# First tiles of the first two experts limited to blocks 0 to 5 and computed unsplit beside the routing of the last blocks

## The chip, the cores and the metric

The kernel runs on one core of a Trainium2 chip. The metric is the device time of one execution in microseconds (us). Five engines work side by side, each with an instruction queue of its own that is worked off in order: TensorE (PE, matmuls; its weight loads are PEld), VectorE (DVE), ScalarE (ACT), GpSimd (POOL) and SyncE (SP, which issues most transfers). A compiler fixes the order within each queue ahead of time from a timeline that it simulates; on the chip, semaphores hold an instruction until its inputs are there.

## The reference, cut to what matters

One layer: attention and a state-space branch, merged and projected to `x`, then a mixture of experts on the normalised `x`. The change touches the second block only:

```python
def hierarchical_moe(h, ...):                        # 1024 tokens of width 1024
    g_prob, g_idx = top_k(softmax(ht @ w_group_router + group_bias), 1)      # one of 4 groups
    in_group = expert logits of that group                                   # 4 experts
    e_val, e_loc = top_k(softmax(in_group), 2)                               # two experts of 16
    gates = one_hot(e_glob) * g_prob * e_val / sum(e_val)
    a = einsum('td,edf->tef', ht, w_e_gate)          # 1024 -> 256
    u = einsum('td,edf->tef', ht, w_e_up)
    hid = silu(a) * u * gates[:, :, None]
    out = hid.reshape(t, 16 * 256) @ w_e_down        # 256 -> 1024
```

## The kernel before, in words

**Blocks.** The output projection runs over eight blocks of 128 tokens (loop `for b in range(8)`, lines 1225 to 1275). A block has two halves of 512 columns, and a half has eight steps of three matmuls, because a float32 product is made of three products of numbers split into a high and a low part (`woh`/`wol`, `mh`/`ml`). At fixed steps `(half, kb)` of this loop, pieces of the routing of earlier blocks are called: `x1_transpose` (the block's `x`, transposed), `logits` or, for blocks 0 to 5, `pair_logits` and `pair_sum` (two blocks at once, on split numbers), `choose` (the two experts of each token and their weights), `place` (each token's rank within its expert, from the running counts `cum`), `slots` (matmuls of one-hot matrices that add the tokens to the table `slot`) and `h2_store` (the normalised block to DRAM, for gathering).

**Tables.** `slot` holds, for each of 16 positions, columns of 128 token numbers and gate weights. A position is an expert's place in the table: positions 0 to 7 and 8 to 15 are two halves of the experts whose tokens never overlap; positions 0 and 8 belong to experts 0 and 4, known ahead. Ranks above the first 128 go to a second column (a rank over 191 of the first eight positions, over 127 of the others, is moved on by 64, so that the second column of positions 0 to 7 fills rows 0 to 63 and that of 8 to 15 rows 64 to 127). The other positions are sorted by their counts (`key`, `rank`, `OHP`), and the numbers of the experts in that order (`who`, `whoi`, lines 1316 to 1323) are read by SP to load the right weights.

**Tiles.** There are 21 tiles of up to 128 tokens: (0), (0, 8), (8), then (5), (13), (1), (1, 9), (9) and so on. A tile of one position is computed on split numbers (24 matmuls of 512 columns for gate and up, 12 for down, lines 1426 to 1428 and 1468 to 1470); a shared tile takes up to 64 second-column tokens of each of two positions and is computed on float32 as it is (lines 1423, 1464), both halves side by side. Each tile gathers its tokens from DRAM (line 1378, POOL), transposes them (1407), computes, gathers the rows of the output (1389), adds (1471) and scatters them back (1395). A gather of output rows waits for the scatters of those tiles that may hold the same tokens. Tiles (0), (0, 8) and (8) wait for the table of all eight blocks (lines 1290 to 1296).

**Buffers.** `s4` tiles come from a pool of 40 buffers of 4 KB a partition; expert weights take six (`load_expert`, line 1007 and 1011), their split versions twelve (`split`, lines 100 and 101). `x4` tiles come from a pool of seven during the blocks. Weights of position 0 are loaded after block `LB`, those of position 8 after the blocks.

Of the kernel before, what the change touches and what calls it, by code (L numbers as in the profile page):

```python
# [19 lines left out]
D = 1024  # L20
# [5 lines left out]
LB = 6  # L26
# [11 lines left out]
def hybrid_layer(ctx, tc, a, out):  # L38
# [1007 lines left out]
    rbias, rbias0 = rtile("rbias", [128, 24]), rtile("rbias0", [128, 24])  # L1046
# [4 lines left out]
    wr, wr0 = rtile("wr", [128, KB, 24]), rtile("wr0", [128, KB, 24])  # L1051
# [24 lines left out]
    pool.tensor_scalar(num[:, 8:], num[:, 8:], 4.0, None, op0=OP.subtract)  # L1076
    kofs = rtile("kofs", [128, 16])
# [18 lines left out]
    def x1_transpose(b, hf):  # L1096
        if b >= 6 and hf == 0:
            X1T[b] = x4([128, KB, 128], F32, "x1T")
        if b < 6 and b % 2 == 0:
# [5 lines left out]
        if b >= 6:  # L1105
            act.activation(X1T[b][:, 4 * hf:4 * hf + 4].rearrange("p k c -> p (k c)"), p, AF.Copy)
            return
        hi, lo = [t[:, :, 128 * (b % 2):128 * (b % 2) + 128] for t in X1T[b - b % 2, hf]]
        p = p.rearrange("p (k c) -> p k c", k=4)
        act.activation(hi, p, AF.Copy)  # L1110
        dve.tensor_sub(lo, p, f(hi))

    def logits(b, hf):
        if hf == 0:
            LG[b] = pst("lg", 2)
        for kb in range(4 * hf, 4 * hf + 4):
            pe.matmul(LG[b][:, :24], X1T[b][:, kb], wr[:, kb], start=(kb == 0), stop=(kb == 7))
# [61 lines left out]
    def place(b):  # L1179

        OH, mk, wx = CH.pop(b)
        r = LG.pop(b)[:, 32:48]
# [41 lines left out]

    for b in range(8):
# [3 lines left out]
        for half in range(2):  # L1229
            c = slice(512 * half, 512 * half + 512)  # L1230
            p = pst("mm", 3)
            for kb in range(KB):
# [6 lines left out]
                if step == (0, 6) and b:  # L1239
                    if b == 7:  # L1240
                        logits(6, 1)
                        choose(6)
                    h2_store(b - 1)
                if step == (1, 4):
                    x1_transpose(b, 0)
                if b >= 2 and b % 2 == 0:
# [8 lines left out]
                if b >= 3 and b % 2:  # L1255
# [5 lines left out]
                if step == (1, 5) and b == 7:  # L1261
                    place(6)
                if step == (1, 7) and b >= 6:
                    logits(b, 0)
# [16 lines left out]
    slots(7)  # L1281
    h2_store(7)

    sl = const.tile([128, 432], F32, name="sl")
    id0 = const.tile([128, 3], I32, name="id0")
    gh0 = const.tile([128, 3], F32, name="gh0")
    tx, te = rtile("tx", [128, 3]), rtile("te", [128, 3])
    dve.tensor_scalar(te[:, :1], slot[:, :1], 0.0, 4096.0, op0=OP.is_equal, op1=OP.mult)  # L1290
    dve.scalar_tensor_tensor(id0[:, :1], slot[:, :1], -1.0, te[:, :1], op0=OP.add, op1=OP.add)
    dve.tensor_copy(sl, slot)
    dve.tensor_add(tx[:, 1:2], sl[:, 1:2], sl[:, 73:74])
    dve.tensor_copy(tx[:, 2:3], sl[:, 72:73])
    dve.tensor_scalar(te[:, 1:], tx[:, 1:], 0.0, 4096.0, op0=OP.is_equal, op1=OP.mult)
    last_dve = dve.scalar_tensor_tensor(id0[:, 1:], tx[:, 1:], -1.0, te[:, 1:], op0=OP.add, op1=OP.add)
    cntp = pst("lg", 2)
    pe.matmul(cntp[:, :16], ones, cum, start=True, stop=True)
    key = const.tile([128, 16], F32, name="key")
    cnt = const.tile([128, 16], F32, name="cnt")  # L1300
    dve.scalar_tensor_tensor(key, cntp[:, :16], 8.0, kofs, op0=OP.mult, op1=OP.add)
    dve.tensor_sub(cnt, cntp[:, :16], eoff)
    ph4.close()


    ov = ctx.enter_context(tc.tile_pool(name="ovt", reuse_waits="tile", bufs=1))
    rank = ov.tile([128, 2, 7], F32, name="rank")
    ph5 = ExitStack()
    sm = ph5.enter_context(tc.tile_pool(name="sm", reuse_waits="tile", bufs=1))
    ps = ph5.enter_context(tc.tile_pool(name="ps5", reuse_waits="tile", bufs=1, space=bass.MemoryType.PSUM))  # L1310
    og = [sm.tile([128, D], F32, name=f"og{i}") for i in range(3)]
# [3 lines left out]
    gt, OHP = sm.tile(HE, F32, name="gt"), sm.tile(HE, F32, name="OHP")  # L1315
# [4 lines left out]
    who, whoi = sm.tile([128, 14], F32, name="who"), sm.tile([128, 14], I32, name="whoi")  # L1320
# [4 lines left out]
    dve.tensor_add(sl[:, 144:288], sl[:, 144:288], sl[:, 288:])  # L1325
    slv = sl[:, :288].rearrange("p (x h e c) -> p x h e c", x=2, h=2, c=9)
    prod, part = sm.tile([128, 2, 14, 7], F32, name="prod"), sm.tile([128, 2, 2, SHARED - 1], F32, name="part")
    tab = sm.tile([128, 2, 13 + SHARED], F32, name="tab")
# [9 lines left out]
    idp, tep = sm.tile([128, 13 + SHARED], I32, name="idp"), sm.tile([128, 13 + SHARED], F32, name="tep")  # L1338
    dve.tensor_scalar(tep, tab[:, 0], 0.0, 4096.0, op0=OP.is_equal, op1=OP.mult)
    dve.scalar_tensor_tensor(idp, tab[:, 0], -1.0, tep, op0=OP.add, op1=OP.add)  # L1340
    dve.tensor_copy(gh0[:, 0::2], slv[:, 1, :, 0, 0])
    dve.tensor_add(gh0[:, 1:2], sl[:, 145:146], sl[:, 217:218])
# [12 lines left out]
    def split_expert(e):  # L1355
# [5 lines left out]
        for t in RAW[e][1]:  # L1361
# [4 lines left out]
    tiles = [((p,), id0[:, c:c + 1], gh0[:, c:c + 1]) if len(p_) == 1 else (p_, id0[:, c:c + 1], gh0[:, c:c + 1])  # L1366
             for c, p_ in enumerate(((0,), (0, 8), (8,))) for p in p_[:1]]
# [7 lines left out]
    acc = []  # L1375
# [6 lines left out]
    def access(n, ins):  # L1382
        for m, o in acc:
            if m != n and not any(x // 8 == y // 8 and x != y for x in tiles[m][0] for y in tiles[n][0]):
                tc.declare_no_dep(ins.ins, o.ins, reason="other rows of the output")
        acc.append((n, ins))

    def gather_out(n):
        access(n, pool.indirect_dma_start(
# [4 lines left out]
    def scatter(n):  # L1394
        access(n, pool.indirect_dma_start(
# [81 lines left out]
    for p in seq[:2]:  # L1477
        if p not in RAW:
            RAW[p] = load_expert(number(p))
    xg.append(s4([128, D], F32, "xg"))  # L1480
    gather(0)
    last = gather(1)
    with tc.issue_after(last.ins):
        for t in xg[2:] + og:
            pool.memset(t, 0.0)
    with tc.issue_after(last_act.ins), tc.issue_after(last_dve.ins):
        parts = split_expert(seq[0])
        for _ in range(4):
            next(parts)
        xpose(0)  # L1490
        for _ in parts:
            pass
    for n in range(NT + 1):
        if n < NT:
# [6 lines left out]
            if not alone:  # L1501
                bg.append(split_expert(es[1]))
            elif i + 1 < 16 and not (i % 2 == 0 and es[0] < SHARED):
                bg.append(split_expert(seq[i + 1]))
# [5 lines left out]
            gate_up(n, (lambda: hid_t(n - 1)) if n else (lambda: None), pump)  # L1510
        else:
            hid_t(n - 1)
        if n:
            down(n - 1, pump)
        while bg:
            pump()
# [5 lines left out]
    ps = ph6.enter_context(tc.tile_pool(name="ps6", reuse_waits="tile", bufs=1, space=bass.MemoryType.PSUM))  # L1522

# [138 lines left out]
```

## Time and profile before

| | before |
|---|---|
| median of 3 runs | 1060.28 us (1060.02 to 1061.85) |
| the profiled execution | 1057.99 us |
| its span, first to last instruction | 1056.2 us |
| TensorE busy | 977.8 us, 93% of the span |
| VectorE, ScalarE, POOL busy | 616.4, 435.9, 252.9 us |
| mean granted TensorE clock | 0.969 of full |
| moved by DMA | 153.24 MB |

The span is what the trace shows; the execution's own time is 1.8 us longer, and the runs that were timed without a profile have a median 2.3 us above it. A busy TensorE is not TensorE at its peak, since matmuls are pipelined and their ends are modelled: the price of a matmul within a run of them is read from the distance between two starts.

### The profile page before, as it was taken

To read this page: it belongs to the slowest core of one execution; us is meant where nothing else is said; L and a number is where in the kernel's file an instruction comes from. 1 tells how busy PE (TensorE), PEld (TensorE's weight loads), DVE (VectorE), ACT (ScalarE), POOL (GpSimd) and SP (SyncE) were. 2 spreads that over 40 slices of the span, in tenths; PEclk is the share of its full clock that TensorE was granted. 3 is DMA by queue.
4 is the path that set the end of the run, shared out by engine and by line. 5 is a ranking of instruction groups with operands and counts; after the bars stand their busy time and mean duration, and the time that the engine had idled before them with its cause. 6 is when DMAs were issued, how large, how long until landed. Compare 5 with 4: busy or idle time off the path is not lost.

```text
span 1056.2 us, 14525 instructions
## 1 busy us (share of the span) xinstructions
PE 977.8 (93%) x5135; PEld 755.8 (72%) x5135; DVE 616.4 (58%) x1341; ACT 435.9 (41%) x757; POOL 252.9 (24%) x312
## 2 busy tenths in 40 slices
PE   6998899999899999999999999899976989999993
PEld 5786688887677767788888888688853665666551
DVE  5756775874856556252210434826677868788841
ACT  6512215234656566340121223433334546666710
POOL 1199503212000000000000212823335223233132
PEclk9999899999999998999999999999986999999996
DMA  8242214134545261242211112433575998989522
GB/s 277 95 132 82 83 41 122 60 84 126 135 104 126 70 180 31 88 119 64 60 40 31 50 41 85 159 121 119 174 265 199 344 379 281 392 273 365 211 93 101
DMA packets 100267, 153.24 MB, mean 145 GB/s; under 512 B 10421, under 2 KB 59097, under 8 KB 100185
## 3 DMA queue, kind: packets, MB, share of 16 engines
q1 hardware_dynamic: 90968, 126.52, 37.9%
q0 software_dynamic: 9072, 25.18, 6.5%
q8 instruction: 42, 0.69, 0.3%
q10 hardware_dynamic: 144, 0.52, 0.2%
q14 instruction: 41, 0.33, 0.1%
HBM read 121.36 MB, written 28.20 MB: 142 GB/s over the span
## 4 chain that ended last, share of the span: by engine, by line
PE 67%; DMA 8%; DVE 7%; issue 7%; POOL 6%; ACT 2%; SPq 1%; POOLq 0%; DVEq 0%
PE mm L899 22%; PE mm L636 3%; PE mm L638 3%; PE mm L637 3%; PE S L760 3%; PE o L807 3%; PE mm L1234 3%; PE mm L1235 2%; PE mm L1233 2%; PE h L1423 2%; DMA k<-hl 2%; PE pt L792 2%; PE h L1427 2%; PE h L1428 2%; PE h L1426 2%
## 5 line engine op out<-in xcount | busy, mean ns | idle before, releaser
L989 POOL TENSOR_TENSOR t<-t,am 128x512 f32<-128x512 f32 x14 | 21.4, 1548 | 378.4 <-DVE t L988 378.4
L101 DVE TENSOR_TENSOR w1l<-w1r,w1h 128x1024 fp32r<-128x1024 f32 x64 | 76.0, 1220 | 3.9 <-ACT w1h L100 3.9
L636 PE MATMUL mm<-qh,hh 128*128 128x512 f32 x192 | 77.1, 405 | 0.0
L637 PE MATMUL mm<-ql,hh 128*128 128x512 f32 x192 | 76.0, 396 | 0.0
L638 PE MATMUL mm<-qh,hl 128*128 128x512 f32 x192 | 75.4, 394 | 0.0
L970 ACT ACTIVATE tg<-mm,hb 128x512 f32<-128x512 f32 x24 | 16.4, 685 | 122.5 <-PE mm L899 122.5
L101 DVE TENSOR_TENSOR ful<-fur,fuh 128x1024 fp32r<-128x1024 f32 x11 | 13.5, 1225 | 89.4 <-ACT fuh L100 89.4
L100 ACT ACTIVATE w1h<-w1r 128x1024 fp32r<-128x1024 f32 x64 | 64.0, 1056 | 0.0
L773 DVE CUSTOM_DVE_ANT_0 sb<-S,bias 128x640 f32<-128x640 f32 (+4 forms) x64 | 40.8, 654 | 37.4 <-PE S L760 35.8
L899 PE MATMUL mm<-hh,fuh 128*128 128x512 f32 x192 | 59.5, 390 | 1.0 <-DVE yal L816 1.0
L899 PE MATMUL mm<-hh,ful 128*128 128x512 f32 x192 | 59.1, 389 | 0.0
L899 PE MATMUL mm<-hl,fuh 128*128 128x512 f32 x192 | 59.1, 389 | 0.0
L668 POOL TENSOR_TENSOR st<-st,nhalf 128x8 f32<-128x8 f32 x16 | 28.5, 1806 | 115.4 <-DVE st L666 115.4
L775 ACT ACTIVATE sb<-sb,mx 128x640 f32<-128x640 f32 (+4 forms) x64 | 44.2, 692 | 23.2 <-DVE mx L773 18.9
L1234 PE MATMUL mm<-wol,mh 128*128 128x512 f32 x128 | 51.1, 399 | 2.7 <-POOL wol L930 1.6
L1427 PE MATMUL h<-w1l,xh 128*128 128x512 f32 x128 | 52.8, 412 | 0.3 <-DVE w1l L101 0.3
L1426 PE MATMUL h<-w1h,xh 128*128 128x512 f32 x128 | 53.0, 414 | 0.0
L1428 PE MATMUL h<-w1h,xl 128*128 128x512 f32 x128 | 52.1, 407 | 0.0
L1233 PE MATMUL mm<-woh,mh 128*128 128x512 f32 x128 | 50.4, 393 | 1.0 <-ACT woh L929 1.0
L1235 PE MATMUL mm<-woh,ml 128*128 128x512 f32 x128 | 50.4, 395 | 0.0
L793 ACT ACTIVATE pt<-pt 128x512 f32<-128x512 f32 (+1 forms) x72 | 36.6, 520 | 21.3 <-PE pt L792 21.0
L1471 DVE TENSOR_TENSOR og<-y,og 128x512 f32<-128x512 f32 x42 | 27.8, 687 | 28.0 <-DMA og<-out_y,idp 15.8
(404 smaller groups left out, 2521.3 us busy)
## 6 DMA issues: line engine op xcount, KB each, us to landing
w1r<-in_weg SPq DMA_DIRECT2D x64, 256.0 KB
w1r<-in_weu SPq DMA_DIRECT2D x64, 256.0 KB
w2r<-in_wed SPq DMA_DIRECT2D x32, 512.0 KB
fur<-in_w_in SPq DMA_DIRECT2D x11, 512.0 KB
qr<-in_w_in SPq DMA_DIRECT2D x16, 256.0 KB
qs<-hl SPq DMA_DIRECT2D x32, 128.0 KB
k<-hl SPq DMA_DIRECT2D x16, 256.0 KB
hur<-in_w_branch SPq DMA_DIRECT2D x16, 256.0 KB
```

Of the source, the lines that this page charges most:

```text
L100: act.activation(hi, raw, AF.Copy)
L101: dve.tensor_sub(lo, raw, f(hi))
L636: pe.matmul(o[j], hh[kb][:, tsl], wh, start=(kb == 0), stop=False)
L637: pe.matmul(o[j], hh[kb][:, tsl], wl, start=False, stop=False)
L638: pe.matmul(o[j], hl[kb][:, tsl], wh, start=False, stop=(kb == 7))
L899: pe.matmul(p[half], ww[:, kb], hx[kb][:, 512 * half:512 * half + 512], start=(kb == 0 and n == 0), stop=(kb == nk - 1 and n == 2))
L1233: pe.matmul(p, mh[kb][:, tsl], woh[kb][:, c], start=(kb == 0), stop=False)
L1234: pe.matmul(p, mh[kb][:, tsl], wol[kb][:, c], start=False, stop=False)
L1235: pe.matmul(p, ml[kb][:, tsl], woh[kb][:, c], start=False, stop=(kb == 7))
L1426: pe.matmul(pv, hi[:, kb], wh, start=(kb == 0), stop=False)
L1427: pe.matmul(pv, hi[:, kb], wl, start=False, stop=False)
L1428: pe.matmul(pv, lo[:, kb], wh, start=False, stop=(kb == 7))
```

## The change

Blocks 4 and 5 are routed singly, as 6 and 7 were (`PAIRED = 4`). When block 5 is placed, the counts of positions 0 and 8 are raised to 128 if they are lower, so that tokens of blocks 6 and 7 go to the second column. The first tiles of the two positions then hold tokens of blocks 0 to 5 only, and their tables are read while block 7 is projected (`early_tables`). They are gathered, transposed and computed on float32 as it is, with the raw weights, in program order between the routing steps of block 7 and the loop of experts (`early_*`). The sorting of the other experts moves ahead of `slots(7)`. The loop starts with tile 2, the shared tile (0, 8); output rows of tile 3 are gathered behind tile 2's scatter. Weights of position 0 are loaded one block earlier.

```diff
-LB = 6
+PAIRED = 4
+EARLY = 6
+LB = 5
...
-        if b >= 6 and hf == 0:
+        if b >= PAIRED and hf == 0:
...
 def place(b):
...
         dve.tensor_add(cum, cum, mk)
+        if b == EARLY - 1:
+            n2 = LG_[:, 48:50]
+            pe.matmul(n2, ones, cum[:, 0:16:8], start=True, stop=True, skip_group_check=True)
+            bump = rtile("bump", [128, 2])
+            dve.scalar_tensor_tensor(bump[:1], n2[:1], -1.0, full[:1], op0=OP.mult, op1=OP.add)
+            dve.scalar_tensor_tensor(cum[:1, 0:16:8], bump[:1], 0.0, cum[:1, 0:16:8], op0=OP.max, op1=OP.add)
...
+    def early_tables():
+        te, tg = rtile("tee", [128, 2]), rtile("tge", [128, 2])
+        v = slot.rearrange("p (x e c) -> p x e c", x=3, c=9)[:, :, 0:16:8, 0]
+        dve.tensor_scalar(te, v[:, 0], 0.0, 4096.0, op0=OP.is_equal, op1=OP.mult)
+        dve.scalar_tensor_tensor(ide, v[:, 0], -1.0, te, op0=OP.add, op1=OP.add)
+        for i in range(2):
+            pool.indirect_dma_start(out=xg[i], in_=h2d[:128 * EARLY], ...)
...
+    def early_xpose(i):
+        XE[i] = (s4 if i else x4)([128, KB, 128], F32, "xT")
+        ... eight transposes of xg[i], two copies by ScalarE
+    def early_gate_up(i, after=None):
+        w = RAW[8 * i][0]
+        ...
+        for kb in range(KB):
+            with tc.issue_after(after.ins) if after is not None and kb > 1 else nullcontext():
+                pe.matmul(p.rearrange("p (g c) -> p g c", g=2), x[:, kb], w[kb // 2][:, :, kb % 2],
+                          start=(kb == 0), stop=(kb == 7))
+        ... gate and up as in gate_up, with ghe
+    def early_hid_t(i):
+        ... two transposes, one copy by ScalarE
+    def early_out(i):
+        OG[i] = s4([128, D], F32, "oge")
+        pool.memset(OG[i], 0.0)
+        g = pool.indirect_dma_start(out=OG[i], in_=out[:128 * EARLY], ...)
+    def early_down(i):
+        ... four matmuls on RAW[8 * i][1], two sums into OG[i], one scatter
...
+                if b > PAIRED:
+                    if step == (0, 1) and b > PAIRED + 1:
+                        slots(b - 2)
+                        if b - 2 == EARLY - 1:
+                            early_tables()
+                    if step == (1, 5):
+                        place(b - 1)
+                if b == 7 and step == (1, 1):
+                    early_xpose(0)
...
+    RAW[8] = load_expert(4)
+    for i in range(2):
+        early_out(i)
     x1_transpose(7, 1)
-    logits(7, 1)
+    early_gate_up(0, logits(7, 1))
     slots(6)
     last_act = choose(7)
+    early_xpose(1)
     place(7)
+    ... counts, key, rank, who, whoi (moved up)
+    slots(7)
+    h2_store(7)
+    early_hid_t(0)
+    early_gate_up(1)
+    early_down(0)
+    ... the tables of the other tiles
+    early_hid_t(1)
+    early_down(1)
...
-    gather(0)
-    last = gather(1)
+    gather(2)
+    last = gather(3)
...
-    for n in range(NT + 1):
+    for n in range(2, NT + 1):
...
-            gather_out(n)
+            if n != 3:
+                gather_out(n)
...
+        if n == 3:
+            gather_out(n)
```

## Rows read from the trace of the kernel before

**Rows 1.** The page's chain that ended last, by engine.
```profile
PE 67%; DMA 8%; DVE 7%; issue 7%; POOL 6%; ACT 2%; SPq 1%; POOLq 0%; DVEq 0%
```

**Rows 2.** Stretch: length, busy PE, PEld, DVE, ACT, POOL, clock, DMA share, GB/s.
```profile
780.00:790.00 10.00, 4.42 (x30) 3.23 (x29) 9.89 (x55) 3.78 (x7) 4.95 (x6) 0.81 0.77 299
790.00:800.00 10.00, 3.22 (x7) 1.36 (x7) 8.87 (x57) 3.99 (x5) 2.34 (x3) 0.50 0.14 38
800.00:810.00 10.00, 5.59 (x18) 4.30 (x19) 10.00 (x24) 3.69 (x5) 8.92 (x8) 0.50 0.61 172
840.00:870.00 30.00, 27.39 (x124) 21.81 (x123) 21.99 (x28) 14.63 (x20) 9.72 (x9) 0.94 1.01 386
890.00:920.00 30.00, 29.21 (x142) 21.68 (x140) 27.09 (x35) 17.69 (x25) 10.31 (x9) 1.00 1.02 368
930.00:1010.00 80.00, 80.00 (x381) 53.29 (x378) 66.96 (x84) 48.44 (x68) 22.34 (x16) 1.00 0.78 275
```

**Rows 3.** Instructions in order of time, TensorE: start, duration, engine, line, [idle before].
```profile
782.03 0.63 PE L1104 MATMUL tr<-ident,xr 128*128 128x128 f32 x4 [0.24 <-DVE cum L1189]
...
802.26 1.94 PE L1407 MATMUL tr<-ident,xg 128*128 128x128 f32 x8 [5.59 <-DMA xg<-h2d,id]
...
804.03 0.80 PE L1426 MATMUL h<-w1h,xh 128*128 128x512 f32 x1
...
815.23 2.79 PE L1423 MATMUL h<-w1r,xT 128*64 128x512 f32 x10
```

**Rows 4.** Instructions in order of time, TensorE: what its matmuls cost.
```profile
151.68 0.61 PE L507 MATMUL inc<-U,Tt 128*128 128x128 f32 x4
...
813.30 0.39 PE L1426 MATMUL h<-w1h,xh 128*128 128x512 f32 x1
...
814.00 0.39 PE L1426 MATMUL h<-w1h,xh 128*128 128x512 f32 x1
...
872.24 3.65 PE L1423 MATMUL h<-w1r,xT 128*64 128x512 f32 x16
```

**Rows 5.** Instructions in order of time, TensorE: logits of a pair and of one block.
```profile
758.37 0.28 PE L1126 MATMUL lg<-x1h,wrs 128*48 128x256 f32 x1
...
758.83 0.28 PE L1126 MATMUL lg<-x1h,wrs 128*48 128x256 f32 x1
...
769.66 0.62 PE L1136 MATMUL lg<-i,lgT 48*128 48x24 f32 x4
770.21 1.07 PE L1117 MATMUL lg<-wr,x1T 128*128 128x24 f32 x8
```

**Rows 6.** Instructions in order of time, POOL and VectorE during the last routing.
```profile
786.13 2.34 POOL L1221 TENSOR_TENSOR h<-h,grow 128x1024 f32<-128x1024 f32 x1 [0.90 <-ACT h L1220]
...
786.49 2.00 DVE L1194 TENSOR_SCALAR lin<-lin 128x2 f32<-128x2 f32 x1
...
797.36 1.29 POOL L1378 DMA_INDIRECT xg<-h2d,id  x1 [8.89 <-DVE id L1291]
...
798.22 0.15 DVE L1296 SCALAR_TENSOR_TENSOR id<-tx,te 128x2 int32<-128x2 f32 x1
```

**Rows 7.** Instructions in order of time: output rows of the first unshared tile.
```profile
841.91 1.01 POOL L1395 DMA_INDIRECT out_y<-og,id  x1 [0.31 <-issue]
...
851.89 0.99 POOL L1389 DMA_INDIRECT og<-out_y,idp  x1 [5.27 <-DMA out_y<-og,id]
...
859.51 1.29 DVE L1471 TENSOR_TENSOR og<-y,og 128x512 f32<-128x512 f32 x2 [2.99 <-DMA og<-out_y,idp]
...
860.35 0.47 PE L1468 MATMUL y<-w2h,hih 128*128 128x512 f32 x1 [2.31 <-ACT w2h L100]
```

**Rows 8.** Instructions in order of time: counts, expert numbers, first numbered weights.
```profile
792.92 0.17 DVE L1301 SCALAR_TENSOR_TENSOR key<-lg,kofs 128x16 f32<-128x16 f32 x1
...
802.89 0.74 DVE L1323 CAST whoi<-who 1x14 int32<-1x14 f32 x1
...
804.43 0.36 SPq L1007 DMA_DIRECT2D w1r<-in_weg  x1
```

More of the change, by code (lines that the diff above doesn't have):

```diff
@@ L2 @@
 from collections import deque
-from contextlib import ExitStack
+from contextlib import ExitStack, nullcontext
 import concourse.bass as bass
@@ L1116, in logits @@
         for kb in range(4 * hf, 4 * hf + 4):
-            pe.matmul(LG[b][:, :24], X1T[b][:, kb], wr[:, kb], start=(kb == 0), stop=(kb == 7))
+            mm = pe.matmul(LG[b][:, :24], X1T[b][:, kb], wr[:, kb], start=(kb == 0), stop=(kb == 7))
+        return mm
     def pair_logits(b, hf):
@@ L1223, in h2_store @@
         X1.pop(b)
+    ide = const.tile([128, 2], I32, name="ide")
+    ghe = const.tile([128, 2], F32, name="ghe")
+    def early_tables():
[4 more added lines that the diff above has]
+        for i in range(2):
+            pool.indirect_dma_start(
+                out=xg[i], out_offset=None, in_=h2d[:128 * EARLY],
+                in_offset=bass.IndirectOffsetOnAxis(ap=ide[:, i:i + 1], axis=0),
+                bounds_check=128 * EARLY - 1, oob_is_err=False)
+        dve.tensor_copy(tg, v[:, 1])
+        dve.tensor_add(ghe, tg, v[:, 2])
@@ new lines, in hybrid_layer, with access @@
+    XE, HE_, OG = {}, {}, {}
+    acc = []
+    def access(ps_, ins):
+        for other, o in acc:
+            if other != ps_ and not any(x // 8 == y // 8 and x != y for x in other for y in ps_):
+                tc.declare_no_dep(ins.ins, o.ins, reason="other rows of the output")
+        acc.append((ps_, ins))
+    def early_xpose(i):
+        XE[i] = (s4 if i else x4)([128, KB, 128], F32, "xT")
+        for hf in range(2):
+            p = pst("tr", 2)
+            for j in range(4):
+                kb = 4 * hf + j
+                pe.transpose(p[:, 128 * j:128 * j + 128], xg[i][:, 128 * kb:128 * kb + 128], ident)
+            act.activation(XE[i][:, 4 * hf:4 * hf + 4].rearrange("p k c -> p (k c)"), p, AF.Copy)
@@ new lines, in early_hid_t @@
+    def early_hid_t(i):
+        t, h = HE_.pop(i)
+        p = pst("tr", 2, n=256)
+        for j in range(2):
+            pe.transpose(p[:, 128 * j:128 * j + 128], t[:, 256 + 128 * j:384 + 128 * j], ident)
+        HE_[i] = h
+        act.activation(h, p, AF.Copy)
+    def early_out(i):
+        OG[i] = s4([128, D], F32, "oge")
+        pool.memset(OG[i], 0.0)
+        g = pool.indirect_dma_start(out=OG[i], out_offset=None, in_=out[:128 * EARLY],
+                                    in_offset=bass.IndirectOffsetOnAxis(ap=ide[:, i:i + 1], axis=0),
+                                    bounds_check=128 * EARLY - 1, oob_is_err=False)
+        access((8 * i,), g)
@@ new lines, in early_down @@
+    def early_down(i):
+        h = HE_.pop(i)
+        for half in range(2):
+            c = slice(512 * half, 512 * half + 512)
+            p = pst("mm", 3)
+            for k in range(2):
+                pe.matmul(p, h[:, 128 * k:128 * k + 128], RAW[8 * i][1][k][:, c], start=(k == 0), stop=(k == 1))
+            dve.tensor_add(OG[i][:, c], p, OG[i][:, c])
+        access((8 * i,), pool.indirect_dma_start(
+            out=out[:128 * EARLY], out_offset=bass.IndirectOffsetOnAxis(ap=ide[:, i:i + 1], axis=0),
+            in_=OG[i], in_offset=None, bounds_check=128 * EARLY - 1, oob_is_err=False))
@@ L1290, in hybrid_layer @@
[L1290 to L1296, printed above, removed]
@@ L1308, in hybrid_layer @@
[L1308 to L1311, printed above, removed]
     key3 = key.rearrange("p (h e) -> p h e", h=2)[:, :, 1:]
     HE = [128, 2, 7, 7]
-    gt, OHP = sm.tile(HE, F32, name="gt"), sm.tile(HE, F32, name="OHP")
+    gt, OHP, prod = [t.rearrange("p (h q e) -> p h q e", h=2, q=7) if t.shape[1] == 98 else
+                     t.rearrange("p (x q e) -> p x q e", x=2, q=14) for t in
+                     (lambda t: (t[:, :98], t[:, 98:196], t[:, 256:452]))(s4([128, 452], F32, "rank"))]
@@ L1363, in split_expert @@
             yield
-    tiles = [((p,), id0[:, c:c + 1], gh0[:, c:c + 1]) if len(p_) == 1 else (p_, id0[:, c:c + 1], gh0[:, c:c + 1])
-             for c, p_ in enumerate(((0,), (0, 8), (8,))) for p in p_[:1]]
+    tiles = [None, None, ((0, 8), id0, gh0)]
     JS = [0, 5, 1, 6, 2, 7, 3, 4]
@@ L1380, in gather @@
                                 bounds_check=T - 1, oob_is_err=False)
[L1382 to L1386, printed above, removed]
     def gather_out(n):
-        access(n, pool.indirect_dma_start(
+        access(tiles[n][0], pool.indirect_dma_start(
             out=og[n % 3], out_offset=None, in_=out,
@@ L1394, in scatter @@
     def scatter(n):
-        access(n, pool.indirect_dma_start(
+        access(tiles[n][0], pool.indirect_dma_start(
             out=out, out_offset=bass.IndirectOffsetOnAxis(ap=tiles[n][1], axis=0),
@@ L1476, in hybrid_layer @@
     seq = [p for j in JS for p in (j, 8 + j)]
-    for p in seq[:2]:
-        if p not in RAW:
-            RAW[p] = load_expert(number(p))
+    for p in seq[2:4]:
+        RAW[p] = load_expert(number(p))
     xg.append(s4([128, D], F32, "xg"))
-    gather(0)
-    last = gather(1)
+    pool.memset(xg[2], 0.0)
+    gather(2)
+    last = gather(3)
     with tc.issue_after(last.ins):
-        for t in xg[2:] + og:
+        for t in og:
             pool.memset(t, 0.0)
     with tc.issue_after(last_act.ins), tc.issue_after(last_dve.ins):
[L1487 to L1492, printed above, removed]
-    for n in range(NT + 1):
+        xpose(2)
+    for n in range(2, NT + 1):
         if n < NT:
```

87 lines of the change are left out of this document (49 added, 38 removed).

## The prediction

> **What bounds the kernel now.** I read the views in this order: the page's chain of waits, then busy time by stretch, then the order of instructions where a stretch has a hole. The chain that ended last is TensorE for 67% of the span [rows 1]. By stretch it is full nearly everywhere, with one deep hole at 780 to 810 us: TensorE is busy 4.42, 3.22 and 5.59 us of 10 each time, and its granted clock falls from full to 0.5, which is 1.2 GHz instead of 2.4 [rows 2]. Before and behind the hole TensorE is full: busy for all 80 us from 930 to 1010 [rows 2]. The DMA engines are full too in places, with shares of 1.01 and 1.02 in 840 to 870 and 890 to 920, but 0.78 in 930 to 1010 [rows 2]. So TensorE bounds most of the expert loop, and the weights follow closely.
>
> The hole is the routing of the last blocks. TensorE transposes the rest of block 7 at 782.03; then the work goes through logits, choice, ranks and the slot table, one short VectorE instruction after another; the first gathered tile is transposed at 802.26 and the gate-up of the shared tile (0, 8) begins at 815.23 [rows 3]. Nothing is there to compute meanwhile, since every tile of tokens waits for the last block.
>
> **The change part by part.** The sum is made on the profiled run: 1058.0 us with a span of 1056.2. The runs shown have a median of 1060.3, so 2.3 us are added at the end.
>
> *What fills the hole.* In 780 to 810 TensorE is idle for 30 − 13.2 = 16.8 us. Its 8.8 us of work in 790 to 810 ran at half clock [rows 2]; at full clock that is at most 4.4 us shorter. Latencies don't shrink, so I take 3. About 19.8 us can be won, if TensorE always has something ready there.
>
> *What the two tiles cost.* Split, a tile takes 24 matmuls for gate-up and 12 for down. Three of them pass between the starts 813.30 and 814.00, so one costs 0.233 us [rows 4]; 72 for both tiles make 16.8 us. Unsplit, a tile takes 8 and 4 matmuls on float32. The nearest row is gate-up of a shared tile: 16 records in 3.65 us are four steps of the contraction for two experts at half width [rows 4]; two halves run together, so I price a full-width step like a pair, 3.65/4 = 0.91 us. From the other side, four full-width records of 128 columns (two matmuls) take 0.61 us with their last latency [rows 4]; times four for 512 columns that is at most 1.22 each. 24 × 0.91 = 21.9 us (29.3 at the upper end). The edit adds 5.1 us of TensorE work; the transposes stay the same in number. The splits of experts at positions 0 and 8 go as well, on ScalarE and VectorE; neither bounds the loop, so I count nothing for them.
>
> *Blocks 4 and 5 singly.* A single block costs two half-logits of eight records, 1.07 us each [rows 5], so 4.3 us for two blocks. The pair costs 16 matmuls of 256 columns at a start-to-start of 0.115 us (758.37 to 758.83 is four steps), 1.8 us, and four sums in 0.62 [rows 5]. That is 1.8 us more, inside blocks where TensorE has no hole, so on the path. The extra count matmul and the two VectorE operations that raise the running counts are under 0.2 us. One x4 buffer more per block is asked of a pool of seven; TensorE needs the next x only at the end of a half block, so I count nothing (if that cover is gone, it costs one load, 1 to 3 us).
>
> *Ceiling:* 19.8 − 5.1 − 1.8 = 12.9, some 13 us.
>
> *What is moved past which queue.* (a) The early tables and two gathers are put at the start of block 7 and the first transposes one half block later. An issue-to-use time is 797.36 to 802.26, 4.9 us [rows 6, 3]; a half block of 24 matmuls and what lies between is about 7 us, but POOL's 2.34 us multiplication can stand ahead of the gather [rows 6]. TensorE would wait for 0 to 3 us in order; I take 0.5. (b) In the hole the routing chain and the early matmuls share TensorE and VectorE. Today the shared tile's indices are ready just behind 798.22 [rows 6]. The change shifts that by 1.8 (logits), about 2 (the ranking of experts goes ahead of the last slots) and 1 (the early tile's gating); then 4.9 for the gather and 1.8 for transposes and copies (802.26 to 804.03 today): about 810. TensorE has 21.9 us of early matmuls and some 6 us of routing and transposes from 784 on: about 812. The two are nearly tied, so small waits of the in-order queue don't all hide: 0 to 10, I take 2. (c) The first unshared tile (5) must gather rows of the output behind the scatter of (0, 8). Today: scatter issued 841.91, gather 851.89, its sum at 859.51, and TensorE, queued behind it, idle for 2.31 until 860.35 [rows 7]. Today the down products of tiles 0 and 8 (12 and 12 matmuls, 5.6 us) lie beside that wait; they are gone. 0 to 5.6 us, I take 1.5. (d) SP: the first numbered weights go out at 804.43, behind the expert numbers of 802.89, though the counts were ready at 792.92 [rows 8]. The changed order computes the numbers right after the counts, so the loads start some 3 to 6 us earlier; this keeps the loop fed and is not counted as gain.
>
> On VectorE one `lin` instruction took 2.00 us while POOL multiplied from 786.13 to 788.47 [rows 6]. The Trainium skill, page "SBUF — State Buffer", section "Who interferes with whom", says that the port pair shared by VectorE and GpSimd is an exclusive lock and that the later instruction stands still for the whole of the other. That speaks against this change, which puts two memsets and up to six indirect transfers on POOL beside the chain. By that rule, with about 1 us for each of four meetings (an estimate from that page and the 1 us of a gather), the chain would end at 814 instead of 810 and the time would be about 1053.
>
> *Sum:* 13 − 0.5 − 2 − 1.5 = 9 us. 1058.0 − 9 = 1049.0, and 1051 against the median. Behind the loop's start nothing else is new: the tail of gathers and scatters starts when the last gate-ups are through, so it shifts along.
>
> **The rivals.** *The weights bound the loop* (DMA shares of 1.01 and 1.02 [rows 2]). Then TensorE's gain turns into waits for weights, and the time falls only by what the DMA engines win: an earlier first load, 3 to 6 us, and two scatters less in the full stretch, about 2. That gives 1053 to 1056. For it: TensorE already loses 2.6 us in 840 to 870. Against it: 0.78 in 930 to 1010 leaves room to catch up.
>
> *The gather of (0, 8) is queued on POOL behind the early scatters.* These wait for the last early sums, about 812. Gather 1, landing 4.9 and transposes 1.8 put its gate-up at about 820, 8 us later than tied; TensorE stands empty and its clock may fall as it does in 780 to 790 today [rows 2], some 2 us more, while the 2 us taken for small waits are then inside the 8. 1051 + 8 = 1059.
>
> *Slower: the early matmuls run at half clock.* In the hole today the clock is 0.5 [rows 2]. If TensorE begins the hole idle and its clock stays there, 21.9 us of matmuls become 43.8. The gain of 9 turns into a loss of about 9 if half of that delay survives behind the tied chain and 13 if all does: 1069 to 1073. It decides from about 9 of the 21.9 us at half clock. Against it: the first two steps of the early gate-up are free to run before block 7's logits, so TensorE should not go idle for long.
>
> *It does not do what it says*: the queue of TensorE, an order fixed ahead, holds the early matmuls until the routing is through. Then the hole stays and 5.1 + 1.8 are added: 1067.
>
> The overflow loop at the end is not a rival: running the reference's routing gives positions 0 and 8 130 and 105 tokens in blocks 0 to 5 and 51 and 27 in blocks 6 and 7, so their second tiles hold 53 and 27 of 64.
>
> **How the numbers follow.** The forecast of 1051 (1046 to 1056 by itself) has 0.58. Weights as the bound 0.16, the gather behind the scatters 0.12, half clock 0.06, no overlap 0.08. If in addition the waits inside the loop (TensorE idle 2.6 us in 840 to 870, and 0.79 in 890 to 920 [rows 2]) shrink with the earlier loads, the time goes to 1044, which is the low end; the high end, 1062, leaves out the two slow cases. 0.2% is about 2 us, what a measurement here can tell from no change. Faster than 1058.2: the forecast, nearly all of the weights' case and a little of the gather's, 0.75. Within: most of the gather's case and the edges, 0.12. Slower: 0.13.
>
> **What would show it right or wrong.** Right: 780 to 810 is full on TensorE at a clock of 1.0, with float32 matmuls of 512 columns whose records start about 0.45 us apart; the gate-up of (0, 8) starts near 812 to 815 and is followed at once by tile (5); the first numbered weights go out near 800. Wrong: a hole of more than 5 us in front of (0, 8) (gather or chain), VectorE or ScalarE waiting for weights at tiles (5), (13) or (1) (DMA), a granted clock of 0.5 under the early matmuls, or a wait in block 7 ahead of the early transposes. The prediction fails most likely where the fixed order of the in-order queues differs from what the landings allow.

## The result and the profile after

The changed kernel takes 1073.5 us (median; 1070.6 to 1074.4), the kernel before 1060.2 on the same chip: a ratio of 1.0123, with a 95% interval of 1.0095 to 1.0152. It is slower by 1.2%, where 1051 us and a range up to 1062 were forecast. The profiled execution took 1072.86 us with a span of 1071.0, 14.8 more than the span of before.

Busy time by stretch of the changed kernel, in the columns of [rows 2]:

```profile
780.00:790.00 10.00, 3.26 (x13) 1.92 (x12) 5.86 (x38) 0.59 (x3) 4.27 (x4) 0.80 1.00 371
790.00:800.00 10.00, 9.43 (x46) 6.75 (x46) 2.17 (x15) 5.33 (x10) 2.92 (x2) 0.86 0.42 168
800.00:810.00 10.00, 9.51 (x29) 4.48 (x28) 6.62 (x34) 1.52 (x4) 0.00 (x0) 1.00 0.10 37
810.00:820.00 10.00, 9.39 (x26) 3.95 (x24) 5.40 (x21) 1.04 (x3) 2.91 (x3) 1.00 0.78 242
820.00:830.00 10.00, 0.15 (x1) 0.00 (x0) 0.69 (x1) 0.00 (x0) 6.93 (x8) 0.67 1.03 404
830.00:840.00 10.00, 3.81 (x16) 2.66 (x18) 0.26 (x1) 2.08 (x4) 0.99 (x1) 0.50 0.66 255
870.00:880.00 10.00, 4.50 (x21) 3.44 (x20) 5.37 (x8) 2.47 (x5) 3.94 (x2) 0.91 0.88 337
```

Where before had one hole at 780 to 810, TensorE now has two. The middle is full, as forecast: 9.4 to 9.5 of 10 us from 790 to 820. But there is idle time ahead of it (780 to 790) and a new hole of 16 us behind it (820 to 836), in which TensorE has nothing and its granted clock falls to 0.5. The chain that ended last says the same; beside [rows 1] TensorE has lost 12 points to "issue", DMA and POOL:

```profile
PE 55%; issue 15%; DMA 11%; POOL 9%; DVE 6%; ACT 2%; SPq 1%; POOLq 0%; DVEq 0%
```

The steps of both holes, TensorE in order of time (columns of [rows 3]; L1272 is the early transposes, L1108 block 7's, L1281 the early gate-up, L1222 the slot tables of block 6, at 785.16, and of block 7, at 811.29, L1189 the rank of block 7, L1387 its count, L1506 and L1522 tile (0, 8)):

```profile
785.16 0.46 PE L1222 MATMUL slot<-R,L 128*128 128x432 f32 x1 [3.12 <-DVE L L1214]
786.15 0.73 PE L1222 MATMUL slot<-R,L 128*128 128x432 f32 x1 [0.53 <-DVE R L1216]
789.79 1.94 PE L1272 MATMUL tr<-ident,xg 128*128 128x128 f32 x8 [2.92 <-DMA xg<-h2d,ide]
791.57 1.11 PE L1108 MATMUL tr<-ident,xr 128*128 128x128 f32 x4
792.48 2.03 PE L1281 MATMUL mm<-w1r,xT 128*128 128x512 f32 x4
794.34 0.60 PE L1108 MATMUL tr<-ident,xr 128*128 128x128 f32 x4
...
797.71 5.40 PE L1281 MATMUL mm<-w1r,xT 128*128 128x512 f32 x12
802.94 0.60 PE L1272 MATMUL tr<-ident,xg 128*128 128x128 f32 x4
803.38 0.17 PE L1189 MATMUL lg<-mk,tri 128*128 128x16 bf16 x1
...
804.07 3.70 PE L1281 MATMUL mm<-w1r,xT 128*128 128x512 f32 x8 [0.49 <-ACT xT L1273]
807.61 0.17 PE L1387 MATMUL lg<-cum,ones 128*128 128x16 bf16 x1
807.63 3.68 PE L1281 MATMUL mm<-w1r,xT 128*128 128x512 f32 x8
...
811.29 0.63 PE L1222 MATMUL slot<-R,L 128*128 128x432 f32 x2
...
836.19 2.89 PE L1506 MATMUL tr<-ident,xg 128*128 128x128 f32 x12 [16.03 <-DMA xg<-h2d,id]
839.00 3.54 PE L1522 MATMUL h<-w1r,xT 128*64 128x512 f32 x12
```

Block 7 is transposed in two halves, at 791.57 and 794.34. The second half, with which its routing goes on, was at 782.03 before [rows 3]. In TensorE's queue it now stands behind the slot table of block 6, which waits 3.12 and 0.53 us for VectorE, behind the early transposes, which wait 2.92 us for a gather, and behind four records of the early gate-up. Rank, count and slot table of block 7 each stand behind a batch of early matmuls. For two of them VectorE's rows tell how long (L1173 makes what the rank needs, L1216 what the slot table needs):

```profile
800.33 0.17 DVE L1173 TENSOR_TENSOR mk<-OH 128x16 bf16<-128x16 f32 x1
...
807.03 0.61 DVE L1216 TENSOR_SCALAR R<-i,lin,wx 128x144 fp32r<-128x144 f32 x2
```

The rank's input is there at 800.50 and its matmul starts at 803.38, 2.9 us later; the slot table's at 807.64 and 811.29, 3.6 us later. Gate-up of the tile (0, 8) starts at 839.00 instead of 815.23 [rows 3].

The third step is on POOL. VectorE has the table of tile (0, 8) ready at 813.91 (the end of its instruction), but its gather (`xg<-h2d,id`) goes out 13 us later, POOL in order of time:

```profile
816.78 1.07 POOL L1314 DMA_INDIRECT out_y<-oge,ide  x1 [18.04 <-DMA w1r<-in_weu]
818.16 1.03 POOL L1483 DMA_INDIRECT xg<-h2d,idp  x1 [0.30 <-issue]
819.19 2.75 POOL L1584 MEMSET og<- 128x1024 f32 x3
822.11 0.99 POOL L1483 DMA_INDIRECT xg<-h2d,idp  x1 [0.17 <-issue]
823.10 0.97 POOL L1579 MEMSET xg<- 128x1024 f32 x1
824.24 1.03 POOL L1314 DMA_INDIRECT out_y<-oge,ide  x1 [0.17 <-issue]
825.57 1.02 POOL L1488 DMA_INDIRECT og<-out_y,id  x1 [0.30 <-issue]
826.89 0.99 POOL L1483 DMA_INDIRECT xg<-h2d,id  x1 [0.31 <-issue]
```

Two scatters, two gathers of later tiles, four memsets and a gather of output rows go first.

**The account.** The second half of block 7's transposes is 12.3 us later. From there to the table it takes 19.6 us (794.34 to 813.91) instead of 16.3 (782.03 to the end of the table's instruction in [rows 6]): 3.2 more. From the table to gate-up it takes 25.1 us (13.0 until POOL issues the gather, 9.3 landing, 2.8 transposes) instead of 16.9: 8.2 more. That is 23.8. When the kernel before reached this gate-up it still had 12.0 us of its tiles 0 and 8 to compute, which are done here, so 11.8 us are lost. The remaining 3.0 come later, for the most part at 870 to 880, where TensorE stands for 5.50 us behind the output rows of the tile that follows (0, 8).

### The profile page after: what moved, and what is told of

It reads as the page before. It is cut to its first block, busy times and chain, and to the rows that moved or that the text cites. A ratio compares the mean times of both kernels' runs of the same rounds, so it can differ in the third digit from the quotient of the medians.

```text
span 1071.0 us, 14449 instructions
## 1 busy us (share of the span) xinstructions
PE 979.3 (91%) x5124; PEld 752.6 (70%) x5124; DVE 599.0 (56%) x1322; ACT 424.2 (40%) x744; POOL 251.2 (23%) x314
## 4 chain that ended last, share of the span: by engine, by line
PE 55%; issue 15%; DMA 11%; POOL 9%; DVE 6%; ACT 2%; SPq 1%; POOLq 0%; DVEq 0%
PE mm L901 22%; DMA og<-out_y,idp 4%; PE mm L638 3%; PE mm L640 3%; PE mm L639 3%; PE S L762 3%; PE o L809 2%; PE mm L1327 2%; PE mm L1328 2%; DMA k<-hl 2%; PE mm L1326 2%; PE pt L794 2%; POOL out_y L1494 2%; POOL xg L1483 1%; DMA hl<-hl 1%
## 5 line engine op out<-in xcount | busy, mean ns | idle before, releaser
L103 DVE TENSOR_TENSOR w1l<-w1r,w1h 128x1024 fp32r<-128x1024 f32 x56 | 66.1, 1218 | 3.7 <-ACT w1h L102 3.0
L102 ACT ACTIVATE w1h<-w1r 128x1024 fp32r<-128x1024 f32 x56 | 55.8, 1056 | 0.0
L1526 PE MATMUL h<-w1l,xh 128*128 128x512 f32 x112 | 45.1, 402 | 0.3 <-DVE w1l L103 0.2
L1570 DVE TENSOR_TENSOR og<-y,og 128x512 f32<-128x512 f32 x38 | 25.1, 685 | 35.9 <-DMA og<-out_y,idp 17.2
L1525 PE MATMUL h<-w1h,xh 128*128 128x512 f32 x112 | 45.1, 403 | 0.0
L1527 PE MATMUL h<-w1h,xl 128*128 128x512 f32 x112 | 43.9, 392 | 0.0
```

Of the source, the lines that this page charges most:

```text
L102: act.activation(hi, raw, AF.Copy)
L103: dve.tensor_sub(lo, raw, f(hi))
L1525: pe.matmul(pv, hi[:, kb], wh, start=(kb == 0), stop=False)
L1526: pe.matmul(pv, hi[:, kb], wl, start=False, stop=False)
```

## Experiments

For the comparison each trace is cut into three stages: the start of the out-projection, from there to the first gate-up of tile (0, 8), and from there to the end. The start differs by itself, between 666 and 673 us, so only the other two columns are compared. Kernels without early tiles have work of tiles 0 and 8 left at the cut, in each of them the same 48 split matmuls and 12 transposes; their price, 12.0 us (of which 48 times 0.233 are 11.2), is moved across the cut here. Each row of stages is one profiled execution. Executions of one kernel scatter, the kernel before from 1052.8 to 1062.9 us in 27 of them, so a difference of 1 or 2 us between two rows says little. Ratios are against the kernel before on the same chip.

| kernel | ratio, 95% interval | to gate-up | to the end |
|---|---|---|---|
| before (two traces) | 1 | 158.2, 157.0 | 229.0, 227.2 |
| changed | 1.0123 (1.0095 to 1.0152) | 170.1 | 232.0 |
| TensorE's order mended | 1.0040 (1.0017 to 1.0063) | 163.2 | 229.9 |
| POOL's order mended | 1.0026 (1.0003 to 1.0048) | 155.8 | 230.2 |
| both | 0.9918 (0.9888 to 0.9948) | 150.6 | 225.9 |
| weights late | 1.0100 (1.0070 to 1.0130) | 165.5 | 231.1 |
| all three | 0.9915 (0.9886 to 0.9944) | 148.0 | 233.6 |
| blocks 4, 5 singly alone | 0.9935 (0.9908 to 0.9961) | 156.9 | 223.9 |
| the same, weights of 0 earlier | 0.9936 (0.9915 to 0.9957) | 157.3 | 224.1 |
| blocks 2 to 7 singly | 0.9992 (0.9975 to 1.0009) | 157.7 | 229.9 |
| before, 10 fills | 1.0014 (0.9989 to 1.0040) | 159.6 | 226.3 |
| before, 16 fills | 0.9980 (0.9953 to 1.0007) | 160.4 | 223.5 |

### 1. TensorE's order

```diff
-                if b == 7 and step == (1, 1):
-                    early_xpose(0)
...
-    early_gate_up(0, logits(7, 1))
+    lg7 = logits(7, 1)
+    with tc.issue_after(lg7.ins):
+        early_xpose(0)
+        early_gate_up(0)
```

> The changed kernel with one thing moved: on TensorE the transposes and the gate-up product of the early tile of expert 0 stand behind block 7's second x1 transposes and its logits, not ahead of them. Theory A (TensorE's order): block 7's routing stood 9.5 us behind the gather of the early tile, so its transposes start at about 783 us rather than 791.6 and the table of the tile (0,8) is ready about 8 us earlier than the 813.9 of the changed kernel; but that tile's gather still stands behind the early scatters on POOL, so some of this is caught there. Time 1064 to 1070. Theory B (POOL's order and the slow gather carry the loss, the routing's delay has cover): within 2 us of the changed kernel, 1071 to 1075. Theory C (the routing's delay is the whole loss): 1058 to 1062.

1062.4 us, a ratio of 1.0040: 0.8% or 8.8 us off the changed kernel. The time lies between theories A and C, 1.6 us below A's range and 0.4 above C's; the trace speaks for A. The second half of block 7's transposes starts at 784.55 and the table is ready at 806.34; counted from the start of the out-projection (669.8 here, 668.9 in the changed kernel) that is 10.7 and 8.5 us earlier. But its gather leaves POOL at 822.40, now 16.1 us after the table instead of 13.0, because the early scatters wait for TensorE as before; then it lands in 7.7 us instead of 9.3. So 8.5 us won in the routing brought gate-up forward by 6.9.

### 2. POOL's order

```diff
+    xg.append(s4([128, D], F32, "xg"))       # ahead of the loop over early_out
+    pool.memset(xg[2], 0.0)
...
     last_dve = dve.scalar_tensor_tensor(id0, tx, -1.0, te, op0=OP.add, op1=OP.add)
+    g2 = pool.indirect_dma_start(out=xg[2], ..., ap=id0[:, 0:1], ...)
+    with tc.issue_after(g2.ins):
+        early_scatter(0)
...
     early_down(1)
+    with tc.issue_after(g2.ins):
+        early_scatter(1)
...
-    gather(2)
-    last = gather(3)
+    with tc.issue_after(g2.ins):
+        last = gather(3)
```

> The changed kernel with one thing moved: on POOL the gather of the tile (0,8) is queued directly behind its table of tokens; the two early scatters and the gather of tile 3 come after it. Theory A (POOL's order holds the gather for 13.0 us after its table is ready): issued at about 814.5 rather than 826.9, gate-up of (0,8) starts 9 to 12 us earlier than 839.0, time 1061 to 1065. Theory B (the gather's landing is bounded by the weights that stream beside it, so an earlier issue lands little earlier): 1068 to 1073. Theory C (the rest of TensorE's work was late anyway, by block 7's routing): 1070 to 1074.

1060.7 us, a ratio of 1.0026: 10.3 us off. Theory A holds, with a little more than it gave: gate-up starts at 824.62 in the trace, 14.4 us earlier than 839.00. The table is ready at 813.79 and the gather leaves at 814.07. It still takes 9.0 us to the first transpose:

```profile
823.05 1.64 PE L1517 MATMUL tr<-ident,xg 128*128 128x128 f32 x8 [3.03 <-DMA xg<-h2d,id]
```

but only 3.03 us of that are idle time, because the early matmuls cover the rest.

### 3. Both orders

The two edits together.

> The changed kernel with both moves: block 7's transposes and logits ahead of the early tiles on TensorE, and the gather of (0,8) ahead of the early scatters on POOL. Theory A (both orders carry the loss, and what is left of the change is worth about what the sum of the prediction gave): the table of (0,8) at 804 to 808, its gather landed by 815 to 818 beside TensorE's early work, 1048 to 1056. Theory B (the change itself doesn't pay: unsplit tiles, the slow gather and the output rows eat the hidden hole): 1058 to 1064, no better than before.

1049.7 us, a ratio of 0.9918. Theory A holds, and the two effects add up, as far as the intervals tell: 8.8 and 10.3 apart, 21.7 together. Busy time by stretch of this kernel:

```profile
780.00:790.00 10.00, 6.77 (x41) 5.22 (x39) 9.27 (x59) 3.54 (x12) 6.38 (x7) 0.93 0.97 333
790.00:800.00 10.00, 8.74 (x27) 5.15 (x28) 6.92 (x28) 3.07 (x4) 2.44 (x1) 0.73 0.65 260
800.00:810.00 10.00, 9.87 (x29) 4.58 (x27) 4.20 (x22) 1.36 (x3) 3.63 (x4) 1.00 0.31 86
810.00:820.00 10.00, 8.65 (x28) 4.03 (x26) 3.67 (x6) 1.64 (x4) 4.33 (x6) 1.00 1.00 365
820.00:830.00 10.00, 10.00 (x52) 4.44 (x51) 8.31 (x9) 8.23 (x11) 3.47 (x3) 1.00 1.04 403
```

The hole behind the early tiles is gone (820 to 830 is full), and 6.0 us of idle time are left in 780 to 820.

### 4. The early gather without the weights beside it

```diff
+    sig = dram.tile([1, 8], F32, name="sig")
+    landed = sp.dma_start(sig, xg[1][:1, :8])
+    with tc.issue_after(landed.ins):
-    RAW[8] = load_expert(4)
+        RAW[8] = load_expert(4)
```

> The changed kernel with one thing moved: the loads of expert 4's weights wait on SP's queue until the early gathers have landed, so that these have the DMA queues for themselves. Theory A (the early gather's 9.0 us from issue to first transpose is contention with those weights): it lands in 5 to 6 us, the early transposes start at 786 to 787 us rather than 789.8, block 7's transposes follow 3 to 4 us earlier, and most of that reaches the end: ratio to the kernel before 1.007 to 1.010. Theory B (the gather takes that long by itself): still 8 to 9 us, ratio 1.011 to 1.015. Theory C (the weights then come too late for the second early tile): TensorE waits for them before that tile's gate-up, ratio above 1.012.

1068.8 us, a ratio of 1.0100. Theory A holds for the landing. The DMA view gives us from issue to landing of the two early gathers, in the changed kernel and then in this one:

```profile
xg<-h2d,ide POOLq DMA_INDIRECT x2, 9.6
```

```profile
xg<-h2d,ide POOLq DMA_INDIRECT x2, 5.7
```

The same transfer is 3.9 us quicker when the weights are not in flight. Not all of that need be the weights: the two gathers of output rows (`oge`), issued right behind the early gathers in the changed kernel (783.72 and 785.02), also go out later here, at 800.03 and 801.41, and no run parts the two. The time falls by 2.4 us only; TensorE's order also came out a little different here, with the slot table of block 6 behind the early transposes.

### 5. All three, and the count ahead of the early gate-up

```diff
     with tc.issue_after(lg7.ins):
         early_xpose(0)
-        early_gate_up(0)
...
-    pe.matmul(cntp[:, :16], ones, cum, start=True, stop=True)
+    counted = pe.matmul(cntp[:, :16], ones, cum, start=True, stop=True)
+    early_gate_up(0, counted)
```

> The kernel with both orders mended, the late loads of expert 4's weights, and the first early tile's gate-up (all but its first two matmuls) behind the count of block 7. Theory A (the slow early gather still costs the mended kernel some 2.7 us of idle TensorE and a half-clock stretch): 2 to 4 us faster than the kernel with both orders mended, ratio to the kernel before 0.987 to 0.990. Theory B (TensorE's early work is long enough to cover it, the end is set later): 0.990 to 0.994. Theory C (the late weights hold up tile 8): 0.994 or more.

1049.1 us, a ratio of 0.9915: theory B, no faster than with both orders alone. The part up to gate-up did get shorter, by 2.6 us to 148.0, as theory A said. But the stage behind it took 233.6 us instead of 225.9. The tiles and their weights are the same; what differs is the order of TensorE's instructions there (by line and tile names, 717 of its 922 records follow each other in the same sequence). In the trace the granted clock is 0.85, 0.84 and 0.83 in 840 to 850, 850 to 860 and 950 to 960, behind short stands of TensorE, and 1.00 from 820 to 1020 with both orders alone. That the order is the cause of all of the 7.7 us is not shown by this pair: the weights also come at other times.

### 6. Blocks 4 and 5 singly, alone

```diff
+PAIRED = 4
-        if b >= 6 and hf == 0:
+        if b >= PAIRED and hf == 0:
... (and so on in x1_transpose and the block loop, as in the change, with two constants of the router in another pool; no early tiles)
```

> The kernel before with one part of the change alone: blocks 4 and 5 are routed singly (their logits unsplit, one block at a time), no early tiles. The prediction priced this at +1.8 us: 1061.5 to 1062.5. A rival (the routing of single blocks also shortens the last blocks' chain or fills TensorE's idle): 1059 to 1060.5. A rival on the other side (the chain of block 7 meets the later tables of blocks 4 and 5): 1063 to 1066.

1051.0 us, a ratio of 0.9935: 7.8 us faster than before, outside of all three expectations. The out-projection, from its first to the start of its last matmul of this line, does take 112.2 us instead of 110.3:

```profile
L1234 PE MATMUL mm<-woh,mh x128: 387/389/797, 666.9 to 779.1; 128*128 128x512 f32 x128
```

1.9 us more, so the price of 1.8 us was right. The routing of block 7 gives it back: its transposes start 15.3 us ahead of the first gather before, 13.0 here (780.76 to 793.73), since VectorE no longer has tables of blocks 4 and 5 in hand. Up to gate-up nothing is lost (156.9 against 158.2 and 157.0). The rest of the gain lies in the expert stage, 223.9 us instead of 229.0 and 227.2, which this edit doesn't touch.

### 7. What sets the expert stage

Four kernels and a second trace of before ask why. Blocks 2 to 7 singly (`PAIRED = 2`):

> The kernel before with blocks 2 to 7 routed singly, no early tiles. Theory A (blocks 4 and 5 routed singly gain because their routing no longer lies in front of block 7's on VectorE, while a pair routed singly costs TensorE 1.9 us): another pair, far from the end, only costs: 1.5 to 2.5 us slower than with blocks 4 and 5 alone, ratio to the kernel before 0.995 to 0.998. Theory B (routing singly is itself cheaper than in pairs, wherever): faster again, ratio 0.987 to 0.992.

The kernel before again:

> The kernel before, unchanged, a second trace of it. If the stage up to the first gate-up of the tile (0,8) is repeatable, its distance from the start of the out-projection is 146.2 us again, within 0.5. If the expert stage behind it varies by itself, its 241.0 us differ here by 1 to 4 us; if it repeats within 0.5 us, the 5.0 us that it is shorter with blocks 4 and 5 routed singly belong to that edit.

Blocks 4 and 5 singly, weights of position 0 earlier (`LB = 5`):

> Blocks 4 and 5 routed singly and the weights of position 0 loaded one block earlier: all of the change but the early tiles. The order of TensorE in the expert stage is that of the kernel with blocks 4 and 5 routed singly. Theory A (the order sets the stage): about 236 us for the stage and 1050 to 1053 us in all, as without the earlier load. Theory B (that kernel's time was a chance of the transfers): 1056 to 1062.

And the kernel before with idle work on VectorE ahead of the first table, ten times and sixteen times:

```diff
+    for _ in range(10):
+        dve.memset(sl, 0.0)
     dve.tensor_scalar(te[:, :1], slot[:, :1], 0.0, 4096.0, op0=OP.is_equal, op1=OP.mult)
```

> The kernel before with ten extra fills of the tile sl on VectorE ahead of the table of the first tiles: some 2 to 5 us more on the chain, nothing else. The planned order of TensorE in the expert stage is that of the kernel before. Both theories: its stage from the first gate-up of the tile (0,8) to the end stays at 239 to 241 us. It is the control of the next run.

> The same with sixteen fills, 1 to 3 us more on the chain than ten. The planned order of TensorE in the expert stage is now nearly the one of the kernel with blocks 4 and 5 routed singly. Theory A (the 3 to 5 us that the kernel with single blocks is faster in the expert stage come from that planned order, not from the routing): the stage takes 235 to 237 us here, and in spite of the six further fills the time is 0 to 4 us below that with ten. Theory B (the order is not it): 239 to 242 us, and the time 1 to 3 us above that with ten.

Blocks 2 to 7 singly: 1058.6 us, no gain left; the order of TensorE's instructions in the expert stage is that of the kernel before, record for record, and the stage takes 229.9. The loss against blocks 4 and 5 alone is larger than theory A gave, since theory A did not have the order in it. The second trace of before differs from the first by 1.2 us up to gate-up (more than expected) and by 1.8 behind it. The earlier load changes nothing: 1051.5 us and 224.1, with the same order as blocks 4 and 5 alone. The last pair speaks for the order. With ten fills it is that of before: 1060.0 us, 226.3 (a little under what was expected). With sixteen it is nearly that of blocks 4 and 5 alone (971 of 982 records in the same sequence): 1055.1 us, 223.5. More work on the chain, and 4.9 us less in all by the medians (3.9 by the means, with an interval of 1.5 to 6.2). The line of the first gate-up matmuls and the span give the stage of this kernel: 1050.6 less 815.1 is 235.5, of which 12.0 are the tiles 0 and 8.

```profile
L1425 PE MATMUL h<-w1r,xT x160: 592/592/644, 815.1 to 1002.2; 128*64 128x512 f32 x160
```

The traces show one place where the order tells. Length, busy TensorE, granted clock, DMA share and GB/s of 850 to 870 in the kernel before, with ten fills and with sixteen:

```profile
850.00:870.00 20.00, 17.39 (x74) 0.91 1.00 386
850.00:870.00 20.00, 18.33 (x78) 0.91 1.02 394
850.00:870.00 20.00, 18.58 (x88) 1.00 1.04 400
```

In all four traces with the order of before TensorE stands idle for 1.3 to 2.3 us ahead of a down product at 857 to 861 (in [rows 7] the one at 860.35), and its clock is granted at 0.5 for 3.4 us behind that; a second stand of 1.2 to 1.4 us follows at 1020 to 1025. In the three traces with the other order the clock is 1.00 throughout 850 to 870, the first stand is gone, and the second is gone or 0.6 us. So the planned order of the expert stage goes with 2 to 6 us (223.5 to 224.1 in one order, 226.3 to 229.9 in the other), and an edit ahead of that stage can flip it.

## Why the prediction was wrong

The sum had the gate-up of (0, 8) near 812 to 815; it came at 839.00. Two steps failed: step (a), priced as a short wait, and the place of (0, 8)'s gather in POOL's queue, which the sum held at nothing and only a rival priced.

**The size of the hole and the price of the tiles held.** The rows at 804.07 and 807.63 are eight records for four full-width matmuls in 3.56 us: 0.89 us each, 0.91 was taken. The out-projection became 1.6 us longer (111.9 instead of 110.3), 1.8 was taken. With all three orders mended the part up to gate-up is 148.0 instead of 158.2 or 157.0: 9.0 to 10.2 us, beside 10.5 in the sum up to there (13 less 0.5 and 2). TensorE's order, POOL's order and the weights beside the gather are what kept the changed kernel from it.

**Step (a), the wait in block 7, failed.** It was bounded by 0 to 3 us and taken at 0.5. The idle time that the gather's landing ended is 2.92 us, just inside; but the second half of block 7's transposes is 12.3 us later, or 10.7 without the out-projection's part. Two things were missed. The landing was priced by a gather of 4.9 us from a stretch where the DMA share was 0.14 to 0.61 [rows 2]; the early gather runs beside the weights of expert 4, at a share of 1.00, and takes 9. And the early transposes that wait for it, block 6's slot table and a part of the early gate-up stand ahead of block 7's own transposes and logits, so the whole remaining chain waits for all of them. Experiment 1 takes the early work out of the way, and the second half starts 114.8 us behind the start of the out-projection instead of 125.4; before it was 113.0. The row that would have told the landing was there: 780 to 790 had a share of 0.77 before [rows 2], with the same weights issued from 773.87 to 780.34.

**Step (b), the small waits, came near its size by luck.** For the chain 3 us of added work and 2 us of waits (of 0 to 10) were taken; it is 3.2 us longer in all. The waits alone are 6.5 us, three times what was taken: rank and slot table, matmuls of 0.2 to 0.6 us, stand 2.9 and 3.6 us behind batches of 3.7 to 5.4 us. The rest of the chain is 3.2 us shorter, since VectorE has the tables of blocks 4 and 5 behind it; experiment 6 shows 2.3 us of that without early tiles. Experiment 1 shows what TensorE's order costs in steps (a) and (b) together: 8.8 us.

**The rival of POOL's queue was the right one and too small.** It had the gather of (0, 8) behind the early scatters, 8 us and 1059. It didn't count what else stands in that queue: each issue is 1.3 us with its gap, the memsets of `og` and `xg` 3.7, and gathers of tiles 3 and later go first. That is 13.0 us, 2.9 until the first early tile's sums let its scatter go and 10.1 for the queue, and 9.3 of landing at a share of 1.03, in place of 4.9. Experiment 2 shows 10.3 us from that order alone. As the rival said, the clock falls to 0.5 at the end of the hole.

**Step (c), output rows, was low.** 1.5 of 0 to 5.6 us were taken. TensorE stands for 5.50 us behind them where it stood for 2.31 [rows 7], 3.2 us more. (The row of before puts its 2.31 down to ScalarE's split of the down weights, `w2h`, not to the sum, whose first half ended at about the same time; how much of it was the output rows' is open.) Scatter, gather and sum are at 862.61, 869.98 and 878.77:

```profile
862.61 1.02 POOL L1494 DMA_INDIRECT out_y<-og,id  x1 [6.09 <-DVE og L1570]
...
869.98 2.00 POOL L1488 DMA_INDIRECT og<-out_y,idp  x1 [0.31 <-issue]
...
878.77 1.29 DVE L1570 TENSOR_TENSOR og<-y,og 128x512 f32<-128x512 f32 x2 [3.79 <-DMA og<-out_y,idp]
```

**Step (d) had the wrong sign.** The first numbered weights go out at 810.43, 6.0 us later than in [rows 8] and not 3 to 6 earlier. The move did what it was for: from the count's matmul to the loads it takes 2.8 us (807.61 to 810.43) instead of 11.7. But the count itself is 14.9 us late.

**The half clock as a rival was not it**: 0.86 and 1.00 in 790 to 810. Nor was "no overlap". Nor did the weights bound the loop: behind 836 TensorE's longest wait for one is 0.3 us. Beside POOL's multiplication a `lin` instruction of VectorE took 2.00 us in the kernel before [rows 6]; beside the early memsets (777.41 to 779.45) one pair of `R` instructions took 1.32 us instead of 0.61, and beside the indirect issues at 780.82 to 786.0 none was more than 0.1 us longer than elsewhere (the same pair of `R` took 0.61). So the 4 us that were worked out from the Trainium skill, page "SBUF — State Buffer", section "Who interferes with whom", for four such meetings did not show: the multiplication and the memsets agree with its lock; beside the indirect issues, to which the prediction carried the rule over, no instruction stood.

**What the sum did not contain** is that the compiler orders the expert stage anew. It was taken as unchanged behind its start. Orders of the same work differ by 2 to 6 us between kernels without early tiles, and by up to 7.7 between the two mended ones. So the 9 us by which the mended kernels beat the kernel before can't be put down to the early tiles alone: against blocks 4 and 5 singly alone, whose order happens to be good, they gain 1.3 to 1.9 us, about as much as the intervals leave open. What early tiles are worth under one and the same order stays open; no run had the order of the stage held fixed across both forms.

## What to carry to other kernels

In an in-order queue, work that is moved into a hole has to stand behind every small step of the chain that ends the hole, on each engine that issues for it; list that queue from the first to the last instruction, issues and memsets included, and ask of the first one when its input lands. Price a gather by a row with the same DMA share as the place it moves to. Where a compiler records the order, run the parts of a change alone and an edit that does nothing useful as a control, before a few microseconds are put down to a cause.

## What the runs showed of the hardware

An indirect gather of 128 rows of 4 KB landed in 5.7 us without weights in flight and in 9.6 beside them and two further gathers. The issue of an indirect transfer mostly held POOL for 1.0 us, and 0.3 us passed to the next, so eight in a row would take some 10 us (an estimate from these two). Elementwise work and memsets on POOL held up VectorE instructions beside them (2.00 us for one of two columns); indirect issues did not. Behind a stand of 1.3 to 2.3 us TensorE's granted clock was 0.5 for 3.4 us in four traces of one order. In the kernel with both orders mended, stands of 1.5 and 2.0 us (at 856.5 and 956.3) left it at 1.00.
